# Down projection of a two-batch encoder: seven products over all tile pairs, two in turns, with splits and operand sums on VectorE

## The chip, the cores and the metric

The kernel runs on one core of one Trainium2 chip. The metric is the device time of one execution in microseconds; the profile is one execution of the same program, and its span is the time from the first to the last instruction. TensorE (PE in the profile) multiplies, VectorE (DVE), ScalarE (ACT) and GpSimd (POOL) do elementwise work, and SyncE (SP) issues nearly all transfers from one queue in order.

## The reference

A one-layer encoder with shared weights runs over two batches of 512 tokens with 1024 channels. Only its last part is touched here:

```python
    h = _rmsnorm(x, norm_ffn_g[l])
    gt, up = jnp.split(h @ w_gu[l], 2, axis=-1)
    x = x + (jax.nn.silu(gt) * up) @ w_down[l]
return _rmsnorm(x, final_norm_g)
```

D_FF is 2816, that is 22 tiles of 128. All is float32.

## The kernel before

**Precision.** A float32 operand is cut into a high part (a cast by ScalarE, L132) and a low part (source minus high part, a subtraction, L133). A product of two operands is three matmuls: high x high, high x low, low x high. `split` does the two instructions; the pair of results is called a block here.

**Two matrix products by Strassen and Winograd.** Gate and up, and then the down projection, are each computed as a 2 x 2 block product with seven products in the place of eight, from sums of the blocks (S of the left factor, T of the right one). In the down projection the left factor A is cut into (batch) x (halves of the 22 inner tiles), the right factor W into (halves of the inner tiles) x (halves of the 1024 outer channels). A *pair* p (0 to 10) is inner tile p together with inner tile p + 11. For a pair, A11 and A21 are the two batches of tile p, A12 and A22 those of tile p + 11, W11 and W12 the two halves of row tile p of w_down, W21 and W22 those of p + 11. The products are P1 = A11 W11, P2 = A12 W21, P5 = S1 T1, P6 = S2 T2, P3 = S4 W22, P7 = S3 T3, P4 = A22 T4, with S1 = A21 + A22, S2 = S1 - A11, S4 = A12 - S2, S3 = A11 - A21, T1 = W12 - W11, T2 = W22 - T1, T3 = W22 - W12, T4 = W21 - T2. One product of one pair is twelve matmuls of 512 columns: four token tiles, three each.

**The loop.** The eleven pairs go in three groups of 3, 4 and 4. In a group the seven products follow one another: P1, P2, P5, P6, P3, P7, P4. At the start of a group `d_raw` loads whole tiles (512 KB) of A, written to DRAM by gate and up as a_d, and of w_down. Functions c5, c6, c3, c7 and c4 make the sums in place on VectorE. Every third block takes its low part from GpSimd (`DLO = 'vvg'`), the others from VectorE. Four PSUM tiles (one per token tile) hold a product; X and Y sets of banks alternate. After a product, its sums leave PSUM: adds on VectorE into x2 (L1568, L1577, L1581, L1586, L1596), copies by ScalarE (L1565, L1572), and adds on GpSimd of these copies into x2 (L1573, L1578, L1582, L1583). In the last group the last product goes token tile by token tile, and `finish` does the last norm of a tile and writes it out.

**What sets the order.** Gate and up emits its products in a written order, one pair of column tiles after another. The program is then ordered for each engine by a scheduler with its own model of costs, so the order on the engines isn't that of the code. A tile with `bufs` buffers is a ring: a load into it waits until the last reader of the buffer's old content is done.

## Time and profile before

| what | us |
|---|---|
| three timed runs | 1886.22, 1885.33, 1880.94 (median 1885.33) |
| the profiled execution: time, span | 1886.2, 1886.2 |
| TensorE matmuls busy | 1748.8 (93%) |
| VectorE, ScalarE, GpSimd busy | 1177.0, 778.2, 785.5 |
| down projection, first matmul to last | 1604 to 1875 |

Times in the profile are from the start of the span. A timeline row has start, duration, engine, line, operation and tiles; a bracket at its end tells how long the engine was idle before it and what ended that. In groups, "x11 | 18.5, 1678" means 11 instructions, 18.5 us in all, 1678 ns each.

### The profile page before, as it was taken

To read this page: it belongs to the slowest core of one execution; us is meant where nothing else is said; L and a number is where in the kernel's file an instruction comes from. 1 tells how busy PE (TensorE), PEld (TensorE's weight loads), DVE (VectorE), ACT (ScalarE), POOL (GpSimd) and SP (SyncE) were. 2 spreads that over 40 slices of the span, in tenths; PEclk is the share of its full clock that TensorE was granted. 3 is DMA by queue.
4 is the path that set the end of the run, shared out by engine and by line. 5 is a ranking of instruction groups with operands and counts; after the bars stand their busy time and mean duration, and the time that the engine had idled before them with its cause. 6 is when DMAs were issued, how large, how long until landed. Compare 5 with 4: busy or idle time off the path is not lost.

```text
span 1886.2 us, 30967 instructions
## 1 busy us (share of the span) xinstructions
PE 1748.8 (93%) x11676; PEld 1372.1 (73%) x11676; DVE 1177.0 (62%) x1947; ACT 778.2 (41%) x1512; POOL 785.5 (42%) x1081
## 2 busy tenths in 40 slices
PE   6999999999999998899989998799999999778897
PEld 6887766777777775566658897588888888666675
DVE  6623554636445366877875557755555555898887
ACT  5534423343433436565643334333333333334345
POOL 3112436274463735251022136643333332647477
PEclk8999999999999998999999999899999999989998
DMA  4354443434434333220456630122222223430502
GB/s 166 125 171 152 117 115 85 121 88 113 114 87 119 88 104 105 62 54 17 168 199 204 190 101 12 45 90 90 78 90 79 89 79 118 173 112 1 178 1 89
DMA packets 174390, 197.44 MB, mean 105 GB/s; under 512 B 101600, under 2 KB 113248, under 8 KB 174240
## 3 DMA queue, kind: packets, MB, share of 16 engines
q1 hardware_dynamic: 173376, 193.95, 32.5%
q8 instruction: 92, 1.51, 0.3%
q10 hardware_dynamic: 720, 0.98, 0.2%
q14 instruction: 58, 0.48, 0.1%
q0 software_dynamic: 144, 0.52, 0.1%
HBM read 139.05 MB, written 56.36 MB: 104 GB/s over the span
## 4 chain that ended last, share of the span: by engine, by line
PE 64%; DVE 14%; DMA 8%; POOL 6%; issue 4%; ACT 2%; SPq 1%; DVEq 0%; POOLq 0%; ACTq 0%
PE pgC L125 9%; PE pj_gt L125 7%; PE pgB L125 6%; PE pgA L125 6%; PE pj_rkv L125 5%; PE s L125 2%; PE pdc L125 2%; PE pab L125 2%; PE pav L125 2%; DMA wor<-in_w_out 2%; PE sc L125 2%; PE pdx L125 2%; PE pj_mla L125 2%; POOL lt L839 2%; POOL el L841 2%
## 5 line engine op out<-in xcount | busy, mean ns | idle before, releaser
L839 POOL TENSOR_TENSOR lt<-lane,el 128x126 f32<-128x126 f32 (+22 forms) x248 | 94.6, 381 | 39.9 <-DMA lane<-nt_d 21.4
L841 POOL TENSOR_TENSOR el<-el,lt 128x126 f32<-128x126 f32 (+22 forms) x248 | 97.4, 393 | 19.0
L125 PE MATMUL pab<-yo,wab 128*128 128x512 f32 x384 | 94.5, 400 | 5.9 <-ACT yo L132 3.8
L125 PE MATMUL pj_gt<-h_hi,whi_gt 128*128 128x512 f32 x240 | 99.2, 413 | 0.0
L125 PE MATMUL pj_gt<-h_hi,wlo_gt 128*128 128x512 f32 x240 | 98.9, 412 | 0.2 <-DVE wlo_gt L133 0.2
L125 PE MATMUL pj_gt<-h_lo,whi_gt 128*128 128x512 f32 x240 | 98.1, 409 | 0.0
L1203 POOL TENSOR_TENSOR s<-uraw 128x512 f32<-128x512 f32 x22 | 29.2, 1329 | 158.5 <-DMA uraw<-in_w_gu 158.5
L125 PE MATMUL pwo<-woh,m 128*128 128x256 f32 x512 | 93.6, 283 | 0.0
L125 PEld LDWEIGHTS pab<-yo,wab 128*128 128x128 f32 x384 | 71.2, 190 | 26.3 <-DVE wab L133 4.5
L125 PEld LDWEIGHTS pwo<-woh,m 128*128 128x128 f32 x512 | 80.3, 192 | 0.3
L125 PE MATMUL pj_rkv<-h_hi,wlo_rkv 128*128 128x512 f32 x192 | 78.9, 414 | 0.0
L125 PE MATMUL pj_rkv<-h_lo,whi_rkv 128*128 128x512 f32 x192 | 78.1, 407 | 0.0
L125 PE MATMUL pj_rkv<-h_hi,whi_rkv 128*128 128x512 f32 x192 | 77.3, 403 | 0.0
L125 PE MATMUL pwo<-wol,m 128*128 128x256 f32 x256 | 72.5, 284 | 0.9 <-DVE wol L133 0.9
L1270 DVE TENSOR_TENSOR p<-p,pgC 128x512 f32<-128x512 f32 x22 | 15.1, 687 | 86.6 <-PE pgC L125 86.6
L1050 POOL TENSOR_TENSOR g<-g 128x512 f32<-128x512 f32 x16 | 24.9, 1559 | 93.0 <-DVE g L1048 81.8
L466 POOL TENSOR_SCALAR lut<-lut 128x512 f32<-128x512 f32 x32 | 20.5, 641 | 98.4 <-ACT lut L464 98.1
L919 ACT COPY sva<-s 64x128 f32<-64x128 f32 x64 | 16.5, 258 | 105.8 <-PE s L125 96.5
L920 DVE COPY svb<-s 64x128 f32<-64x128 f32 x64 | 18.8, 294 | 54.2 <-ACT sva L919 36.4
L1213 POOL TENSOR_TENSOR s<-graw,uraw 128x512 f32<-128x512 f32 x22 | 29.2, 1328 | 55.3 <-DVE S_2l L133 3.9
L125 PEld LDWEIGHTS pj_gt<-h_hi,wlo_gt 128*128 128x128 f32 x240 | 45.1, 188 | 9.6 <-DVE wlo_gt L133 0.9
L125 PE MATMUL sc<-kt,qh 128*128 128x512 f32 x128 | 50.9, 466 | 0.6 <-ACT pT L554 0.6
(1732 smaller groups left out, 5773.4 us busy)
## 6 DMA issues: line engine op xcount, KB each, us to landing
graw<-in_w_gu SPq DMA_DIRECT2D x22, 512.0 KB, 3.5
uraw<-in_w_gu SPq DMA_DIRECT2D x22, 512.0 KB, 3.6
araw<-a_d SPq DMA_DIRECT2D x22, 512.0 KB, 5.0
draw<-in_w_down SPq DMA_DIRECT2D x22, 512.0 KB, 4.9
a_d<-a SPq DMA_DIRECT2D x21, 512.0 KB, 3.3
x<-in_x SPq DMA_DIRECT2D x16, 512.0 KB, 8.2
rwkv_in<-lut SPq DMA_DIRECT2D x32, 256.0 KB, 2.1
gate_d<-gtt SPq DMA_DIRECT2D x32, 256.0 KB, 2.5
```

The lines of the kernel that those rows point to most:

```text
L125: pin(nc.tensor.matmul(out, lhsT, rhs, start=start, stop=stop, **kw), n if out.shape[0] > 64 else n / 2)
L466: nc.gpsimd.tensor_scalar(t, t, f, f, op0=ALU.mult, op1=ALU.add)
L839: eng.tensor_mul(lv, lane[:, s, s + 1:].unsqueeze(1).to_broadcast([P, m_, n]), el[:, 0:m_, s].unsqueeze(2).to_broadcast([P, m_, n]))
L841: eng.tensor_add(ev, ev, lv)
L919: nc.scalar.copy(sva[HA, :, c], s2[HA])
L920: nc.vector.tensor_copy(svb[HB, :, c], s2[HB])
L1050: nc.gpsimd.tensor_add(g_[:, 0], g_[:, 0], g_[:, 1])
L1203: vg(ES[min(j, 1)]).tensor_add(s1, a21, a22)
L1213: vg(ES[min(j, 1)]).tensor_sub(s3, a11, a21)
L1270: nc.vector.tensor_add(p1, p1, x_)
```

## The change

The groups go. Each product runs over all eleven pairs, and two products take turns, one pair of the one and then one of the other, on the two bank sets: P1 with P5, P6 with P3, P7 with P2, then P4 alone (its last four pairs token tile by token tile, as before). PSUM keeps P1 + P6 + P7 + P4 in X and P5 + P3 in Y running on, so that there are fewer evictions; the state after P1 and after P5 is copied out by ScalarE as before. S, T and W12 stay in SBUF for all pairs (11 buffers each), while the halves of A and W that a product needs are loaded by `d_half` when it needs them, 256 KB each, some of them twice. S3 is made in gate and up and written to DRAM (s3_d). All low parts and sums of the stage are VectorE's; GpSimd keeps eight adds, and its part of `finish`.

```diff
-GROUPS = ((0, 1, 2), (3, 4, 5, 6), (7, 8, 9, 10))
-DLO = 'vvg'
-DSE, DTE = 'v', 'v'
-DBLK = 8
+JP = NFF // 2
+NRH = 10
+DBLK = 7
+NLAST = 4
...
+    s3_d = [dram.tile([P, S], F32, name=f"s3_d{j}") for j in range(JP)]
...
         (nc.sync if j < NFF - 1 else nc.gpsimd).dma_start(a_d[j], a)
+        if j < JP:
+            nc.vector.tensor_sub(p5, a[:, 0], a[:, 1])
+            nc.sync.dma_start(s3_d[j], p5)
...
     lohalf, hihalf = slice(0, 512), slice(512, 1024)
-    cnt = [0, 0]
-    lop = DLO
-
-    def d_raw(tag, src, name):
-        raw = fp.tile([P, D], F32, tag=tag, bufs=2 * max(map(len, GROUPS)), name=name)
+    XB, YB = (3, 0), (1, 2)
+    cnt = [0]
+    def d_half(src, name):
+        raw = fp.tile([P, 512], F32, tag="rh", bufs=NRH, name=name)
         nc.sync.dma_start(raw, src)
         return raw
 
-    def d_block(src, name, first, eng=None):
-        pl, tag, bufs = (fw, "b", NBLK) if first else (fp, "d", DBLK)
+    def resident(tag, name):
+        return fp.tile([P, 512], F32, tag=tag, bufs=JP, name=name)
+    def d_block(src, name):
+        cnt[0] += 1
+        pl, tag, bufs = (fw, "b", NBLK) if cnt[0] % 2 else (fp, "d", DBLK)
         hi = pl.tile([P, 512], F32R, tag=f"{tag}hi", bufs=bufs, name=f"{name}h")
         lo = pl.tile([P, 512], F32R, tag=f"{tag}lo", bufs=bufs, name=f"{name}l")
-        cnt[0] += 1
-        split(hi, lo, src, vg(eng or lop[cnt[0] % len(lop)]))
+        split(hi, lo, src)
         return hi, lo
 
+    def banks(which, nm):
+        return [bank(which[t // 2], f"{nm}{t}") for t in range(4)]
+    def mms(ps, l, r, t, first):
+        ts = slice(t * P, (t + 1) * P)
+        mm3x(ps[t], l[0][:, ts], l[1][:, ts], r[0], r[1], start=first, stop=False, skip_group_check=True)
+    def prod_d(ps, l, r, first=False):
+        for t in range(4):
+            mms(ps, l, r, t, first)
+    def turns(fx, fy):
+        fx(0)
+        for p in range(1, JP):
+            fx(p)
+            fy(p - 1)
+        fy(JP - 1)
+    def xs(b, t, h):
+        return x2[b * 4 + t][:, (lohalf, hihalf)[h]]
...
-    fg = None
-    for gi, grp in enumerate(GROUPS):
...
-        def product(nm, ps, lhs, rhs, first, combos=None, touter=False):
-            blk = {}
-
-            def mms(p, t):
-                ts = slice(t * P, (t + 1) * P)
-                l, r = blk[p]
-                mm3x(ps[t], l[0][:, ts], l[1][:, ts], r[0], r[1], start=(first and p == grp[0]), stop=False,
-                     skip_group_check=True)
-            for p in grp:
-                if combos:
-                    combos(p)
-                early_ = gi == 0 and nm == "P1"
-                if early_ and p < 2:
-                    blk[p] = pre["araw"][1 + p], pre["draw"][1 + p]
-                else:
-                    blk[p] = [d_block(src[p], f"{nm}{k}{p}", early_ or touter and p < grp[2], "v" if early_ else None)
-                              for k, src in (("l", lhs), ("r", rhs))]
-                if not touter:
-                    for t in range(4):
-                        mms(p, t)
-            if touter:
-                yield -1
-                for t in range(4):
-                    for p in grp:
-                        mms(p, t)
-                    yield t
-
-        def go(*a, **kw):
-            for _ in product(*a, **kw):
-                pass
-
-        def xs(b, t, h):
-            return x2[b * 4 + t][:, (lohalf, hihalf)[h]]
-
-        SE, TE = vg(DSE), vg(DTE)
-
-        def c5(p):
-            SE.tensor_add(S_[p], A21[p], A22[p])
-            TE.tensor_sub(T_[p], W12[p], W11[p])
-
-        def c6(p):
-            SE.tensor_sub(S_[p], S_[p], A11[p])
-            TE.tensor_sub(T_[p], W22[p], T_[p])
-
-        def c3(p):
-            SE.tensor_sub(S_[p], A12[p], S_[p])
-
-        def c7(p):
-            SE.tensor_sub(A21[p], A11[p], A21[p])
-            TE.tensor_sub(W12[p], W22[p], W12[p])
-
-        def c4(p):
-            TE.tensor_sub(T_[p], W21[p], T_[p])
-        c = banks(0, "pdc")
-        go("P1", c, A11, W11, True)
-        p1 = [fp.tile([P, 512], F32, tag="p1", bufs=4, name=f"dp1{gi}{t}") for t in range(4)]
+    araw, W12, S_, T_ = {}, {}, {}, {}
+    X, Y = banks(XB, "dx"), banks(YB, "dy")
+    def p1_(p):
+        if p == 0:
+            araw[p], w11 = pre["araw"][0], pre["draw"][0][:, lohalf]
+        else:
+            araw[p] = fw_raw(a_d[p].rearrange("p b s -> p (b s)"), f"araw{p}")
+            w11 = d_half(w_down[p][:, lohalf], f"w11_{p}")
+        T_[p] = w11
+        if p < 2:
+            blk = pre["araw"][1 + p], pre["draw"][1 + p]
+        else:
+            blk = d_block(araw[p][:, lohalf], f"dA11_{p}"), d_block(w11, f"dB11_{p}")
+        prod_d(X, *blk, p == 0)
+    def p5_(p):
+        a22 = d_half(a_d[p + JP][:, 1], f"a22_{p}")
+        W12[p] = resident("w12", f"w12_{p}")
+        if p == 0:
+            nc.vector.tensor_copy(W12[p], pre["draw"][0][:, hihalf])
+        else:
+            nc.sync.dma_start(W12[p], w_down[p][:, hihalf])
+        w11, T_[p] = T_[p], resident("t", f"T{p}")
+        S_[p] = resident("s", f"S{p}")
+        nc.vector.tensor_add(S_[p], araw[p][:, hihalf], a22)
+        nc.vector.tensor_sub(T_[p], W12[p], w11)
+        blk = d_block(S_[p], f"dS1_{p}"), d_block(T_[p], f"dT1_{p}")
+        nc.vector.tensor_sub(S_[p], S_[p], araw[p][:, lohalf])
+        prod_d(Y, *blk, p == 0)
+    turns(p1_, p5_)
+    p1 = [fp.tile([P, 512], F32, tag="p1", bufs=4, name=f"dp1{t}") for t in range(4)]
+    p5 = [fp.tile([P, 512], F32, tag="p5", bufs=4, name=f"dp5{t}") for t in range(4)]
+    for t in range(4):
+        nc.scalar.copy(p1[t], X[t])
+    for t in range(4):
+        nc.scalar.copy(p5[t], Y[t])
+    w22 = {}
+    def p6_(p):
+        w22[p] = d_half(w_down[p + JP][:, hihalf], f"w22_{p}")
+        nc.vector.tensor_sub(T_[p], w22[p], T_[p])
+        blk = d_block(S_[p], f"dS2_{p}"), d_block(T_[p], f"dT2_{p}")
+        nc.vector.tensor_sub(W12[p], w22[p], W12[p])
+        prod_d(X, *blk)
+    def p3_(p):
+        a12 = d_half(a_d[p + JP][:, 0], f"a12_{p}")
+        nc.vector.tensor_sub(a12, a12, S_[p])
+        prod_d(Y, d_block(a12, f"dS4_{p}"), d_block(w22[p], f"dB22_{p}"))
+    turns(p6_, p3_)
+    for ps in (X, Y):
         for t in range(4):
-            nc.scalar.copy(p1[t], c[t])
-        go("P2", c, A12, W21, False)
-        for t in range(4):
-            nc.vector.tensor_add(xs(0, t, 0), xs(0, t, 0), c[t])
-        y = banks(1, "pdy")
-        go("P5", y, S_, T_, True, c5)
-        for t in range(4):
-            nc.scalar.copy(p5[t], y[t])
-            nc.gpsimd.tensor_add(p5[t], p5[t], p1[t])
-        x_ = banks(0, "pdx")
-        go("P6", x_, S_, T_, True, c6)
-        for t in range(4):
-            nc.vector.tensor_add(xs(0, t, 1), xs(0, t, 1), x_[t])
-            nc.gpsimd.tensor_add(xs(0, t, 1), xs(0, t, 1), p1[t])
-        go("P3", y, S_, W22, False, c3)
-        for t in range(4):
-            nc.vector.tensor_add(xs(0, t, 1), xs(0, t, 1), y[t])
-            nc.gpsimd.tensor_add(xs(1, t, 1), xs(1, t, 1), p5[t])
-            nc.gpsimd.tensor_add(xs(1, t, 0), xs(1, t, 0), p1[t])
-        go("P7", x_, A21, W12, False, c7)
-        for t in range(4):
-            nc.vector.tensor_add(xs(1, t, 1), xs(1, t, 1), x_[t])
-        for t in product("P4", x_, A22, T_, False, c4, touter=lastg):
-            if t < 0:
-                for i in range(4):
-                    finish(i)
-                continue
-            nc.vector.tensor_add(xs(1, t, 0), xs(1, t, 0), x_[t])
-            finish(4 + t)
-        if not lastg:
-            for t in range(4):
-                nc.vector.tensor_add(xs(1, t, 0), xs(1, t, 0), x_[t])
+            nc.vector.tensor_add(xs(0, t, 1), xs(0, t, 1), ps[t])
+    def p7_(p):
+        s3 = d_half(s3_d[p], f"s3_{p}")
+        prod_d(X, d_block(s3, f"dS3_{p}"), d_block(W12[p], f"dT3_{p}"))
+    Y = banks(YB, "dz")
+    def p2_(p):
+        a12, w21 = d_half(a_d[p + JP][:, 0], f"a12b{p}"), d_half(w_down[p + JP][:, lohalf], f"w21_{p}")
+        blk = d_block(a12, f"dA12_{p}"), d_block(w21, f"dB21_{p}")
+        nc.vector.tensor_sub(T_[p], w21, T_[p])
+        prod_d(Y, *blk, p == 0)
+    turns(p7_, p2_)
+    fg = fwr[0].tile([P, D], F32, tag="raw", bufs=NRAW, name="fg")
+    nc.sync.dma_start(fg, fng)
+    for t in range(4):
+        nc.vector.tensor_add(xs(1, t, 1), xs(1, t, 1), X[t])
+        nc.gpsimd.tensor_add(xs(1, t, 1), xs(1, t, 1), p5[t])
+    for t in range(4):
+        nc.vector.tensor_add(xs(0, t, 0), xs(0, t, 0), Y[t])
+        nc.gpsimd.tensor_add(xs(0, t, 0), xs(0, t, 0), p1[t])
+    def p4_(p):
+        a22 = d_half(a_d[p + JP][:, 1], f"a22b{p}")
+        return d_block(a22, f"dA22_{p}"), d_block(T_[p], f"dT4_{p}")
+    for p in range(JP - NLAST):
+        prod_d(X, *p4_(p))
+    last = [p4_(p) for p in range(JP - NLAST, JP)]
+    for t in range(4):
+        finish(t)
+    for t in range(4):
+        for blk in last:
+            mms(X, *blk, t, False)
+        nc.vector.tensor_add(xs(1, t, 0), xs(1, t, 0), X[t])
+        finish(4 + t)
 
 
 def layout(i):
```

Where the instructions stand now. VectorE at the start of the down projection, from its last row of gate and up (names: l and r in P1l2l are left and right factor, then pair, then l or h for the low or high part; dS1_0l is the low part of S1 of pair 0). Before:

```order
L1271 TENSOR_TENSOR a21_16050<-a21_16050,p1_21_15987 128x512
L133 TENSOR_TENSOR P1l2l_16202<-araw2_16146,P1l2h_16201 128x512
L133 TENSOR_TENSOR P1r2l_16206<-draw2_16148,P1r2h_16205 128x512
L1545 TENSOR_TENSOR S0_16167<-araw0_16111,araw11_16150 128x512
L1546 TENSOR_TENSOR T0_16168<-draw0_16117 128x512
L133 TENSOR_TENSOR P2l0l_16230<-araw11_16150,P2l0h_16229 128x512
L1556 TENSOR_TENSOR araw0_16111<-araw0_16111 128x512
L1557 TENSOR_TENSOR draw0_16117<-draw11_16152,draw0_16117 128x512
L133 TENSOR_TENSOR P2r0l_16234<-draw11_16152,P2r0h_16233 128x512
```

and with the change:

```order
L1272 TENSOR_TENSOR a21_16083<-a21_16083,p1_21_16020 128x512
L1527 COPY w12_0_16213<-draw0_16150 128x512
L1533 TENSOR_TENSOR T0_16215<-w12_0_16213,draw0_16150 128x512
L133 TENSOR_TENSOR dT1_0l_16224<-T0_16215,dT1_0h_16223 128x512
L1532 TENSOR_TENSOR S0_16216<-araw0_16144,a22_0_16211 128x512
L133 TENSOR_TENSOR dB11_2l_16249<-w11_2_16242,dB11_2h_16248 128x512
L133 TENSOR_TENSOR dS1_0l_16220<-S0_16216,dS1_0h_16219 128x512
L1535 TENSOR_TENSOR S0_16216<-S0_16216,araw0_16144 128x512
L133 TENSOR_TENSOR dA11_2l_16245<-araw2_16240,dA11_2h_16244 128x512
L1532 TENSOR_TENSOR S1_16269<-araw1_16195,a22_1_16264 128x512
L1533 TENSOR_TENSOR T1_16268<-w12_1_16266,w11_1_16197 128x512
L1532 TENSOR_TENSOR S2_16322<-araw2_16240,a22_2_16317 128x512
```

The splits of P1 and P2 and the sums of S and T stood there; now the copy of W12 of pair 0, then sums and splits of P5 and P1 in turns. The split of S1 of pair 10, the last operand of P5, stands 88 rows behind the copy.

GpSimd from the last store of gate and up on. Before:

```order
L1272 DMA a_d21_12232<-a21_16050 128x1024
L1583 TENSOR_TENSOR x2_4_10421<-x2_4_10421,dp100_16221 128x512
L133 TENSOR_TENSOR P2l1l_16250<-araw12_16154,P2l1h_16249 128x512
L1583 TENSOR_TENSOR x2_5_10422<-x2_5_10422,dp101_16222 128x512
L1583 TENSOR_TENSOR x2_6_10423<-x2_6_10423,dp102_16223 128x512
L1583 TENSOR_TENSOR x2_7_10424<-x2_7_10424,dp103_16224 128x512
L133 TENSOR_TENSOR P2r2l_16274<-draw13_16160,P2r2h_16273 128x512
L133 TENSOR_TENSOR P5l1l_16322<-S1_16169,P5l1h_16321 128x512
```

with the change:

```order
L1273 DMA a_d21_12232<-a21_16083 128x1024
L1582 TENSOR_TENSOR x2_4_10421<-x2_4_10421,dp50_16750 128x512
L1582 TENSOR_TENSOR x2_5_10422<-x2_5_10422,dp51_16751 128x512
L1582 TENSOR_TENSOR x2_6_10423<-x2_6_10423,dp52_16752 128x512
L1582 TENSOR_TENSOR x2_7_10424<-x2_7_10424,dp53_16753 128x512
L1585 TENSOR_TENSOR x2_0_10417<-x2_0_10417,dp10_16746 128x512
```

The splits and the adds of each group are gone; the adds that stand there now read sums of P7 and P2, five products later.

SP's queue at the same place, where the loads of the stage begin. Before:

```order
L1442 DMA araw1_16142<-a_d1_12212 128x1024
L1442 DMA draw1_16144<-in_w_down 128x1024
L1442 DMA araw2_16146<-a_d2_12213 128x1024
L1442 DMA draw2_16148<-in_w_down 128x1024
L1442 DMA araw11_16150<-a_d11_12222 128x1024
```

with the change:

```order
L1446 DMA w11_1_16197<-in_w_down 128x512
L1446 DMA a22_0_16211<-a_d11_12222 128x512
L1446 DMA w11_2_16242<-in_w_down 128x512
L1182 DMA araw2_16240<-a_d2_12213 128x1024
L1446 DMA a22_1_16264<-a_d12_12223 128x512
L1529 DMA w12_1_16266<-in_w_down 128x512
L1446 DMA w11_3_16295<-in_w_down 128x512
L1446 DMA a22_2_16317<-a_d13_12224 128x512
```

Whole tiles in group order have become halves in the order of use, and between them whole tiles of A (araw), which now share a ring of three buffers with the tiles of gate and up: araw2 takes the buffer of draw0, araw3 that of araw0, and so on by threes.

28 lines of the change are left out of this document (removed).

## The prediction

> **What bounds the kernel now.** I read the busy time by stretches first, for the whole kernel and then for the down projection. Columns: busy microseconds and instruction counts of TensorE (PE), its weight loads, VectorE (DVE), ScalarE (ACT), GpSimd (POOL), then granted clock, DMA share, GB/s.
>
> ```profile
> 1500.00:1600.00 100.00, 100.00 (x443) 82.81 (x442) 55.69 (x70) 34.00 (x58) 32.99 (x24) 1.00 0.28 93
> 1604.13:1875.14 271.01, 230.15 (x937) 183.13 (x935) 233.72 (x265) 110.51 (x209) 172.88 (x111) 0.94 0.23 86
> 1610.00:1620.00 10.00, 5.56 (x24) 3.92 (x22) 9.45 (x11) 5.77 (x11) 6.12 (x5) 0.99 1.03 407
> 1630.00:1640.00 10.00, 10.00 (x46) 8.27 (x45) 10.00 (x16) 3.94 (x7) 6.73 (x3) 1.00 0.00 0
> 1640.00:1650.00 10.00, 6.31 (x27) 4.55 (x26) 10.00 (x7) 2.19 (x5) 9.85 (x7) 1.00 0.01 2
> 1660.00:1670.00 10.00, 9.98 (x35) 8.06 (x36) 10.00 (x10) 3.33 (x7) 9.92 (x7) 0.80 0.41 157
> 1750.00:1760.00 10.00, 8.75 (x39) 6.89 (x37) 8.26 (x7) 6.33 (x12) 9.62 (x6) 1.00 0.61 213
> ```
>
> In the gate and up projection TensorE is full and VectorE half idle. In the down projection (1604 to 1875) it is the other way round. There VectorE does 16 instructions in ten microseconds when GpSimd is moderately busy and 7 when GpSimd is full, and calls itself full both times. The timeline of the two engines side by side shows why (start, duration, instruction):
>
> ```profile
> 1614.26 0.68 DVE L133 TENSOR_TENSOR P2l0l<-araw,P2l0h 128x512 fp32r<-128x512 f32 x1
> 1614.86 1.77 DVE L1556 TENSOR_TENSOR araw<-araw 128x512 f32<-128x512 f32 x1
> 1616.55 1.76 DVE L1557 TENSOR_TENSOR draw<-draw,draw 128x512 f32<-128x512 f32 x1
> 1618.23 1.75 DVE L133 TENSOR_TENSOR P2r0l<-draw,P2r0h 128x512 fp32r<-128x512 f32 x1
> ...
> 1626.64 0.68 DVE L133 TENSOR_TENSOR P2r1l<-draw,P2r1h 128x512 fp32r<-128x512 f32 x1
> 1627.24 0.68 DVE L1545 TENSOR_TENSOR S<-araw,araw 128x512 f32<-128x512 f32 x1
> ...
> 1660.49 1.87 DVE L1577 TENSOR_TENSOR x<-x,pdx 128x512 f32<-128x512 f32 x3
> ```
>
> ```profile
> 1614.65 1.43 POOL L1583 TENSOR_TENSOR x<-x,dp 128x512 f32<-128x512 f32 x1 [1.64 <-ACT dp L1565]
> 1616.05 1.71 POOL L133 TENSOR_TENSOR P2l1l<-araw,P2l1h 128x512 fp32r<-128x512 f32 x1
> 1617.72 5.08 POOL L1583 TENSOR_TENSOR x<-x,dp 128x512 f32<-128x512 f32 x3
> ```
>
> Alone, a split or a sum starts every 0.60 us (1626.64 to 1627.24). Beside a GpSimd instruction it starts every 1.69 us (1614.86 to 1616.55), so one GpSimd instruction takes 1.09 us from VectorE. The adds that read PSUM (L1577, three in 1.87 us, in a stretch with GpSimd 9.92 of 10) aren't stretched. What that does to TensorE, in the chain of waits (first row) and in its timeline:
>
> ```profile
> 1601.41 2.72 PE pgC L125 x12
> ```
>
> ```profile
> 1620.03 0.79 PE L125 MATMUL pdc<-P2r0l,P2l0h 128*128 128x512 f32 x1 [4.48 <-DVE P2r0l L133]
> 1620.62 0.63 PE L125 MATMUL pdc<-P2r0h,P2l0l 128*128 128x512 f32 x1
> 1621.05 0.63 PE L125 MATMUL pdc<-P2r0h,P2l0h 128*128 128x512 f32 x1
> ...
> 1627.38 0.50 PE L125 MATMUL pdc<-P2r1l,P2l1h 128*128 128x512 f32 x1 [2.21 <-DVE P2r1l L133]
> ...
> 1874.75 0.39 PE L125 MATMUL pdx<-P4r10h,P4l10l 128*128 128x512 f32 x1
> ```
>
> Twelve matmuls of 512 columns take 2.72 us, 0.227 each. After 4.48 us of idleness they are 0.43 apart for a while, after 2.21 us they aren't.
>
> The floor of the stage follows. It has 924 matmuls (7 products x 11 pairs x 12), and the last 12 of gate and up lie between them: 78 twelves x 2.72 = 212.2 us. From 1604.1 that ends at 1816.3. It ends at 1875.0 now (the last starts at 1874.75), so at most **58.7 us** can be won. The last norm behind it, from there to the end of the span at 1886.2, is 11.2 us and isn't changed.
>
> **The change part by part.** *GpSimd's work.* Of its 111 instructions between 1604 and 1875, the splits and 40 of 48 adds go; 8 adds, the products by fg and the small powers stay, all in the last product. Before that nothing of GpSimd runs in this stage, so VectorE's rows cost 0.60 us there.
>
> *VectorE's rows.* In the changed order 89 rows (the copy of W12 to the split of S1 of pair 10) lie between its last row of gate and up and the operands of the last P5. That row of gate and up and a ScalarE cast:
>
> ```profile
> 1611.24 0.69 DVE L1271 TENSOR_TENSOR a<-a,p 128x512 f32<-128x512 f32 x1
> 1606.71 0.62 ACT L132 CAST P1l2h<-araw 128x512 fp32r<-128x512 f32 x1 [2.10 <-PE pdc L125]
> ```
>
> VectorE is free at 1611.9. 89 x 0.60 = 53.4 brings it to 1665.3. To this come two casts at the start that it must wait for (2 x 0.65 = 1.3), and loads. The bound is one copy SBUF to SBUF that the trace of before lacks at this size with both ends there; I price it as any row, and it can't cost less than nothing or more than a stretched row's 1.77.
>
> *Loads.* The list of transfers of the whole kernel, and that of the time from 1604 on, when many are under way (KB each, us to landing):
>
> ```profile
> uraw<-in_w_gu SPq DMA_DIRECT2D x22, 512.0 KB, 3.6
> araw<-a_d SPq DMA_DIRECT2D x21, 512.0 KB, 5.1
> ```
>
> SP's queue is in order. araw2 takes the place of draw0, so it waits for T of pair 0 (done at about 1613.0), and everything behind it waits too: a22_1, w12_1, w11_3 and so on. It lands at 1613.3 + 3.6 = 1616.9, is cast by 1617.5, and VectorE wants it at 1616.9: 0.6 us (2.1 by the 5.1 us under load; nothing else is under way then, so I take the first). The pieces behind it arrive 0.65 us apart at the 407 GB/s of the row above (256 KB each); a22_2 is the third half behind it, and VectorE waits another 1.2. Later each araw(p+3) waits for the last use of araw(p); by the rows between, only araw8 is late, by 0.9. In all 2.7. Nine loads of 512 KB and 37 of 256 KB, 14.4 MB, in some 55 us are 262 GB/s. That lies between the 407 and the 213 of the rows above. By 407 the 2.7 stands; by 213 the loads take 68 us, and 12 us are added. I take 2.7, since the 213 was a stretch where the loads waited for buffers, and keep 12 for the range.
>
> Sum of this part: 1665.3 + 1.3 + 2.7 = 1669.3. P5 of pair 9 gets its split two rows before and starts at about 1668.8, P5 of pair 10 follows at 1671.5 and ends at **1674.3**. TensorE alone, from its first P5 at about 1616.2 (five rows and two casts after 1611.9), would need 20 x 2.72 = 54.4 and end at 1670.6: the two engines are nearly level, and VectorE leads by little. That is the lower bound.
>
> *The other five products.* 55 x 2.72 = 149.6 us. VectorE has 164 rows there, 98 us at 0.60, or 7 rows (4.2 us) for every 5.44 us of TensorE in P6 and P3, where they are densest. TensorE is the bound, at 1674.3 + 149.6 = 1823.9. The evictions are 20 adds on VectorE where 60 stood; P6 may write X's banks only after four ScalarE copies, P7 and P4 only after four adds. In the built order two products of the other bank pair (5.44 us) lie between, against 4 x 0.6 us. I cost them at nothing; without that cover they are 2.4 us each, 7.2 in all.
>
> *GpSimd in the last product.* From the end of P7, VectorE has 25 rows of 512 elements (15.0 us), about 1 us of small ones, and up to 16 GpSimd instructions (8 adds, 8 products by fg) that take 1.09 each: 33.4 at most. TensorE gives it 5.44 (two products of P2), 7 x 2.72, and some 2 us until the last block is needed: 26.5. So 0 to 6.9; I take 3, because the products by fg come late, behind ScalarE.
>
> The Trainium skill, SBUF — State Buffer, "Who interferes with whom", says that the pair of ports that VectorE and GpSimd share is locked for a whole instruction and the loser blocks. GpSimd's instruction alone is 1.29 us here, in the groups of the time from 1400 to 1600:
>
> ```profile
> L1203 POOL TENSOR_TENSOR s<-uraw 128x512 f32<-128x512 f32 x10 | 12.9, 1290 | 80.9 <-DMA uraw<-in_w_gu 80.9
> ```
>
> By the page's lock the bound of 6.9 would be 16 x 0.20 = 3.2 us larger. The 1.69 against 0.60 of VectorE's own rows decides.
>
> *Gate and up.* Eleven tile pairs get one subtraction and one 256 KB store more. Their cover:
>
> ```profile
> L1271 DVE TENSOR_TENSOR a<-a,p 128x512 f32<-128x512 f32 x11 | 18.5, 1678 | 0.0
> L1270 DVE TENSOR_TENSOR p<-p,pgC 128x512 f32<-128x512 f32 x11 | 7.6, 687 | 43.9 <-PE pgC L125 43.9
> L1261 DVE TENSOR_TENSOR e<-e,pgB 128x512 f32<-128x512 f32 x10 | 6.9, 687 | 15.6 <-PE pgB L125 15.6
> ```
>
> VectorE waits 4.0 us per pair for TensorE at L1270 and 1.5 at L1261, and the new row takes 0.6 to 1.7 just ahead of the second wait. The store is queued on SP one row later than the store of a and ahead of the next load of uraw, so it holds SP up by no more than the subtraction takes. TensorE has no pause in the stretch from 1500 to 1600 that stands at the top. I cost it at nothing; without that cover it is 11 x 1.77 = 19.5.
>
> *The sum*: 1823.9 + 3.0 + 11.2 = 1838.1, and 1 us for matmuls on half clock after an idle stretch. **1839 us** against the profiled 1886.2, which is 0.9 above the median of the three runs, so 47 us or 2.5%.
>
> The Trainium skill, TensorE: Matmul & The Clock Gate, "HAM oscillation", wants no idle gap over about 3.4 us. The trace agrees: 2.21 us left the clock alone, 4.48 didn't. The changed first part may have two gaps of 3 to 4 us (before P1 of pairs 2 and 4); if the page counts them, each makes some 8 matmuls 0.2 us longer, 3.2 us in a part that VectorE sets anyway.
>
> **The rivals.** *Loads set the first part.* The loads are smaller, more, and chained through buffers. For it: SP's queue waits for VectorE before most of these loads, and the margins are a few microseconds. Against: 407 GB/s in the trace. By the 213 row 12 us more: 1851; with P6's loads late too, up to 1862.
>
> *TensorE without a gap.* VectorE's rows overlap the waits that I added, and the last product's stall vanishes: 1816.3 + 11.2 = 1827.5. For it, only that the engines are nearly level; against, the 4.3 us of operands that have to be made before the first P5.
>
> *VectorE becomes the bound of everything, and it is slower than before.* All 253 rows up to the last split are now on VectorE. If the stretching doesn't come from GpSimd but from ScalarE, or from the transfers, whose share rises, the rows stay at 1.69. 253 x 1.69 = 428 us from 1611.9 is 2040, + 11.2 = 2051. It decides from a mean of (1875.0 - 1611.9) / 253 = 1.04 us per row. Against: at 1614.26 the row is still 0.68, with the DMA at 407 GB/s and ScalarE at work; it stretches when GpSimd starts at 1614.65.
>
> *No change.* The gain is there, but in-order waits of VectorE for block buffers (5 on the left side) take it back: 1886. The five-block lead is 2.5 pairs, 13 us; I find no row that would be waited for that long.
>
> **How the numbers follow.** Forecast, 1832 to 1846: 0.58. Loads, 1846 to 1862: 0.22. No gap, under 1832: 0.10. Slower than before: 0.04. No change, or a part of the gain (above 1862): 0.06, half of it within 0.3% of before, which is about what a measurement of this kernel can tell from no change. That makes faster 0.93, the same 0.03, slower 0.04. The range is 1828 to 1860: it takes in the gapless bound and the loads at 213 GB/s with most of what can follow.
>
> **What would show it.** Right: no GpSimd tensor instruction from about 1612 to the end of P7, VectorE's rows at 0.68, busy share of TensorE near full from the start of P6, and a first part that ends near 1674 with short waits of TensorE on VectorE's splits. Loads: SP waits on VectorE, VectorE idle until araw or a22 lands. Wrong as a whole: rows of VectorE above 1.04 us without GpSimd beside them, or TensorE idle in P6 to P7.

## The result, and the profile after

| | kernel before | changed kernel |
|---|---|---|
| device time, median (lowest to highest) of 4 runs, us | 1885.09 (1880.94 to 1886.22) | 1834.53 (1830.80 to 1838.51) |
| ratio, 95% interval | | 0.9737 [0.9718, 0.9757] |
| the profiled execution: time, span, us | 1886.22, 1886.2 | 1835.74, 1834.0 |
| first P1 matmul starts, us | 1603.97 | 1600.02 |
| last matmul starts, us | 1874.75 | 1825.73 |
| between them | 270.8 | 225.7 |
| from there to the end of the span | 11.4 | 8.3 |

The changed kernel is 2.6% faster: 50.6 us between the medians, where 47 were forecast. Of the 52.2 us between the two spans, 45.1 come from the down projection, 3.2 from what lies behind its last matmul, and 4.0 from the program ahead of it, which has no part in the change (the last section shows that this start moves by itself).

The busy time by stretches of the changed kernel answers to the first table of the prediction (TensorE, its weight loads, VectorE, ScalarE, GpSimd, then granted clock, DMA share, GB/s):

```profile
1600.02:1825.73 225.71, 216.44 (x936) 177.34 (x935) 171.88 (x270) 105.36 (x197) 30.68 (x24) 0.98 0.44 147
1620.00:1630.00 10.00, 7.41 (x32) 5.47 (x30) 10.00 (x18) 4.61 (x9) 0.00 (x0) 1.00 1.04 390
1630.00:1640.00 10.00, 8.97 (x32) 7.25 (x33) 9.54 (x16) 4.46 (x8) 0.00 (x0) 0.83 0.98 362
1640.00:1650.00 10.00, 10.00 (x45) 8.27 (x45) 10.00 (x18) 3.87 (x7) 0.00 (x0) 1.00 0.39 123
1750.00:1760.00 10.00, 10.00 (x46) 8.29 (x45) 6.56 (x10) 4.29 (x8) 0.00 (x0) 1.00 0.45 140
1810.00:1820.00 10.00, 7.81 (x33) 5.83 (x33) 6.30 (x7) 4.20 (x10) 8.25 (x6) 1.00 0.28 110
```

GpSimd does no arithmetic in the stage until P7 is done (its first addition starts at 1787.19). VectorE does 18 rows in ten microseconds in which it calls itself full, where it did 7 beside GpSimd. TensorE is full in every window of ten microseconds from 1640 to 1810, of which two are shown. What it lacks is at the two ends: the waits of TensorE in the whole stage are five (line of the waiting instruction, what it waited for: us, times, longest):

```profile
PE dy L125 <- ACT dS_0h L132: 3.5, 1, 3.5
PE dx L125 <- ACT dA_4h L132: 2.2, 1, 2.2
PE dx L125 <- ACT dA_10h L132: 1.6, 1, 1.6
PE dx L125 <- ACT dA_3h L132: 1.4, 1, 1.4
PE dx L125 <- DVE dA_9l L133: 0.6, 1, 0.6
```

Three of them, 7.1 us, lie in the first part (P1 and P5 in turns), two, 2.2 us, in the last product. The timeline gives the cuts used in all that follows, the first P1, the first P6 and the last matmul: the first part takes 73.6 us, the rest 152.1.

```profile
1600.02 0.39 PE L125 MATMUL dx<-P1drawh,P1arawh 128*128 128x512 f32 x1
...
1673.60 0.39 PE L125 MATMUL dx<-dT_0h,dS_0h 128*128 128x512 f32 x1
...
1825.73 0.39 PE L125 MATMUL dx<-dT_10h,dA_10l 128*128 128x512 f32 x1
```

The chain of waits shows where the first part is late. It goes through one transfer after the other to the cast of the left block of pair 4:

```profile
1612.26 6.04 DMA w<-in_w_down
...
1618.36 5.95 DMA a<-a_d
...
1624.37 5.96 DMA araw<-a_d
...
1630.36 0.63 ACT dA_4h L132
...
1631.03 3.10 PE dx L125 x8
```

No row of VectorE stands in it. Each transfer takes 6 us to land and is issued right when the one ahead in the chain has landed, while the loads run at 390 GB/s (the window from 1620).

### The profile page after: what moved, and what is told of

Read it like the earlier page. It is cut to its first block, busy times and chain, and to the rows that moved or that the text cites. A ratio compares the mean times of both kernels' runs of the same rounds, so it can differ in the third digit from the quotient of the medians.

```text
span 1834.0 us, 31000 instructions
## 1 busy us (share of the span) xinstructions
PE 1734.3 (95%) x11676; PEld 1365.7 (74%) x11676; DVE 1116.9 (61%) x1957; ACT 771.0 (42%) x1496; POOL 642.2 (35%) x992
## 4 chain that ended last, share of the span: by engine, by line
PE 70%; DVE 9%; DMA 8%; POOL 5%; issue 3%; ACT 2%; SPq 1%; DVEq 0%; POOLq 0%; ACTq 0%
PE pgC L125 9%; PE pj_gt L125 8%; PE pgB L125 6%; PE pgA L125 6%; PE pj_rkv L125 5%; PE dx L125 5%; PE dy L125 3%; PE s L125 3%; PE pab L125 2%; PE sc L125 2%; PE pav L125 2%; PE pj_mla L125 2%; DMA wor<-in_w_out 2%; PE o L125 2%; PE gx L125 2%
## 5 line engine op out<-in xcount | busy, mean ns | idle before, releaser
L1203 POOL TENSOR_TENSOR s<-uraw 128x512 f32<-128x512 f32 x22 | 29.3, 1330 | 152.1 <-DMA uraw<-in_w_gu 152.1
L1582 POOL TENSOR_TENSOR x<-x,dp 128x512 f32<-128x512 f32 x4 | 6.3, 1590 | 178.1 <-DVE x L1581 178.1
L125 PEld LDWEIGHTS pj_gt<-h_hi,wlo_gt 128*128 128x128 f32 x240 | 45.1, 188 | 9.5 <-DVE wlo_gt L133 0.8
L125 PEld LDWEIGHTS pj_gt<-h_hi,whi_gt 128*128 128x128 f32 x240 | 45.1, 188 | 8.6
L125 PEld LDWEIGHTS pj_gt<-h_lo,whi_gt 128*128 128x128 f32 x240 | 45.1, 188 | 8.4
```

Source lines behind the costliest of these rows:

```text
L125: pin(nc.tensor.matmul(out, lhsT, rhs, start=start, stop=stop, **kw), n if out.shape[0] > 64 else n / 2)
L1203: vg(ES[min(j, 1)]).tensor_add(s1, a21, a22)
L1582: nc.gpsimd.tensor_add(xs(1, t, 1), xs(1, t, 1), p5[t])
```

## The experiments

The theory: GpSimd's instructions took VectorE's time in the down projection, and the gain is their going. The rivals: the new order and its fewer evictions are the gain; loads, not VectorE, set the first part; each row or GpSimd instruction costs its price wherever it stands. All ratios below are to the kernel before on the same chip, so they compare with 0.9737.

| kernel | median us | ratio [95%] | first part | first P6 to last matmul | whole stage | behind it |
|---|---|---|---|---|---|---|
| changed kernel | 1834.53 | 0.9737 [0.9718, 0.9757] | 73.6 | 152.1 | 225.7 | 8.3 |
| b_splits | 1863.30 | 0.9904 [0.9888, 0.9921] | | | 253.6 | 10.3 |
| b_allv | 1847.56 | 0.9820 [0.9806, 0.9835] | | | 235.0 | 14.2 |
| b_noadds | 1836.84 | 0.9762 [0.9738, 0.9785] | | | 219.9 | 14.8 |
| a_third | 1848.45 | 0.9828 [0.9803, 0.9854] | 86.6 | 149.8 | 236.4 | 11.8 |
| a_dose | 1882.25 | 1.0008 [0.9994, 1.0021] | 73.7 | 197.5 | 271.2 | 8.2 |
| a_paced | 1833.87 | 0.9743 [0.9719, 0.9768] | 73.5 | 152.1 | 225.6 | 8.3 |
| a_dosecp | 1847.81 | 0.9817 [0.9794, 0.9840] | 72.2 | 154.1 | 226.3 | 20.3 |
| a_vdose | 1837.48 | 0.9751 [0.9734, 0.9768] | 74.8 | 152.1 | 226.9 | 8.2 |
| a_noaraw | 1831.43 | 0.9722 [0.9707, 0.9736] | 67.9 | 152.2 | 220.1 | 8.3 |
| a_s2 | 1829.22 | 0.9712 [0.9698, 0.9726] | 67.9 | 152.2 | 220.1 | 8.1 |
| a_adds | 1831.91 | 0.9724 [0.9708, 0.9740] | 72.3 | 149.4 | 221.6 | 8.2 |
| a_both | 1823.04 | 0.9688 [0.9669, 0.9707] | 67.5 | 149.4 | 216.8 | 8.1 |

The stage columns come from one profiled execution each: starts of the first P1, first P6 and last matmul, and the span's end. The first part is the same work in a_dose, a_dosecp, a_paced, a_adds and the changed kernel and takes 72.2 to 73.7 us there, so a difference of 1.5 says nothing. (The two at 72.2 and 72.3 have one stretch of half clock in it, the other three have two; the last section tells why this varies.)

### What the gain is made of: b_splits, b_allv, b_noadds

b_splits moves GpSimd's splits in the kernel before to VectorE, b_allv its additions too. b_noadds is b_allv without the 32 additions of kept sums in the first two groups, so these sums are missing from its output.

```diff
-DLO = 'vvg'
+DLO = 'vvv'
```
```diff
-            nc.gpsimd.tensor_add(p5[t], p5[t], p1[t])
+            nc.vector.tensor_add(p5[t], p5[t], p1[t])
...
-            nc.gpsimd.tensor_add(xs(1, t, 0), xs(1, t, 0), p1[t])
+            nc.vector.tensor_add(xs(1, t, 0), xs(1, t, 0), p1[t])
```
```diff
-            nc.gpsimd.tensor_add(p5[t], p5[t], p1[t])
+            if lastg:
+                nc.vector.tensor_add(p5[t], p5[t], p1[t])
...
```

> The kernel before, with the one edit that every low part of the down projection is made on VectorE (none on GpSimd); its 48 additions stay on GpSimd, the order of the products stays. By my theory (each GpSimd instruction takes 1.09 us from VectorE, which bounds the stage, and a row of VectorE alone costs 0.60) 50 splits go: + 50 x 0.60 - 50 x 1.09 = -24 us, so about 1861 us, within 1855 to 1872 since TensorE bounds some stretches. Rival (the gain lies in the order in turns and in the fewer evictions): no change, 1885, or slower by up to 30 us, since VectorE has 50 rows more.

> The kernel before, with all splits and all 48 additions of the down projection on VectorE, its old order of products and its 60 evictions kept. By my theory 98 GpSimd instructions go: VectorE has some 350 rows x 0.60 = 210 us, level with TensorE's 212, so the stage takes 225 to 235 us in place of 271: 1840 to 1855 us, and what then is left to the changed kernel (5 to 20 us) is the worth of its order and of its 40 evictions less. Rival (GpSimd is all): 1835, the same as the changed kernel. Rival (the order is what counts): above 1870.

> The kernel before with all its work in the down projection on VectorE, in its old order, and with the 32 additions of kept sums of the first two groups left out, so these sums are missing from the output, which isn't the reference's. It asks what the changed kernel's remaining lead over the all-VectorE kernel of the old order is made of (from the first P1 to the last matmul 235.0 against 225.7 us). If VectorE's number of rows sets the stage there, 32 x 0.60 = 19 us of VectorE go and the 15 us that TensorE waits at the starts of products shrink to 6 or less: 225 to 229 us for the stage, about 1840. If the order sets it (each product starts with operands and banks that stand behind the additions of the one before), the 28 evictions still in the way keep the waits: 232 to 235 us, 1845 to 1848.

b_splits came out 18 us under the kernel before (ratio 0.9904), where 24 were expected, and b_allv 34 under it (0.9820): both inside what the theory gave, and both far from the rivals. VectorE has 50 rows more in b_splits and is done sooner. So some 34 of the 50 us are GpSimd leaving the stage, with the old order of the products. In b_allv TensorE's waits stand at the starts of products or one pair behind them, 15 us; the longest two:

```profile
PE pdx L125 <- DVE x L1586: 5.4, 3, 3.5
PE pdx L125 <- DVE P6r0l L133: 3.0, 1, 3.0
```

In b_noadds the first of them is down to 1.6 us (the same line, four lower there), and the four waits that are left make 5.6 us:

```profile
PE pdx L125 <- DVE x L1590: 1.6, 2, 0.9
```

The stage of b_noadds is 219.9 us, less than the forecast 225 to 229, and less than the changed kernel's 225.7. So it is the number of VectorE's rows that stood behind those waits, not the old order: with 32 rows fewer the old order keeps TensorE fuller than the changed kernel does (5.6 us of waits and no stretch of half clock, against 9.3 us and two). Against b_allv the changed kernel is 9.3 us shorter in the stage and 5.9 behind it (8.3 us against 14.2). The 9.3 are put down to its fewer additions and evictions, which accumulating over all eleven pairs makes possible; the changed kernel itself was not run with the old number of them. What the turns as such are worth was not tried alone either.

### What one GpSimd instruction costs: a_dose, a_paced, a_third, a_dosecp

```diff
+    junk = fp.tile([P, 512], F32, tag="fj", bufs=1, name="dose")
+    for i in range(66):
+        nc.gpsimd.tensor_add(junk, p1[i % 4], p5[i % 4])
     turns(p6_, p3_)
```

> The changed kernel with 66 additions on GpSimd added at the start of P6, each of two finished tiles into a scratch tile that nobody reads; no other edit, and the result isn't touched. They run back to back for about 105 us, while VectorE has 78.9 us of work in the 116.8 us of P6, P3, P7 and P2. By my theory each takes 1.09 us from VectorE: 78.9 + 72 = 151, 34 us more than TensorE needs; with the pitch of 1.69 us only some 62 rows are stretched, which gives 27. So 1861 to 1869 us, TensorE idle behind VectorE's splits. If a GpSimd instruction takes its own full time (the Trainium skill, SBUF - State Buffer, "Who interferes with whom": the port pair is locked for a whole instruction), 78.9 + 66 x 1.29 = 164, so 47 more: 1882. Rival (the stretching came from transfers or from ScalarE): 1834.5.

It took all the gain back: 47.7 us over the changed kernel, ratio 1.0008. The timeline of VectorE beside the 66 additions, and the one row of GpSimd:

```profile
1674.07 110.95 POOL L1562 TENSOR_TENSOR dose<-dp,dp 128x512 f32<-128x512 f32 x66 [64.28 <-ACT dp L1544]
...
1679.41 1.78 DVE L133 TENSOR_TENSOR dS_1l<-a,dS_1h 128x512 fp32r<-128x512 f32 x1
1681.11 1.77 DVE L133 TENSOR_TENSOR dB_2l<-w,dB_2h 128x512 fp32r<-128x512 f32 x1
...
1783.81 1.87 DVE L1566 TENSOR_TENSOR x<-x,dy 128x512 f32<-128x512 f32 x3
```

VectorE's rows are 1.70 us apart, so one GpSimd addition takes 1.10 us from it; the prediction had 1.09. The additions that read PSUM (L1566) run at 0.6 us beside it, again as before. The price held, and the sum of 27 to 34 us made with it did not. It set the whole slack of P6 to P2 against the dose, but the dose stands in P6 and P3 alone. There, 108.5 us pass from the first P6 (1674.44) to the first P2 (1782.95), which are 24 twelves or 65 us for TensorE; what slack VectorE has in the rest of P7 and P2 comes too late to help. The Trainium skill, SBUF — State Buffer, "Who interferes with whom", gave + 47, which is the time that came out, but by the same sum over the whole slack. Its lock for a whole instruction would put the rows 0.60 + 1.29 = 1.89 us apart, and they are 1.70; the measured pitch decides.

a_paced puts 22 additions where VectorE has room, spread by what they read:

```diff
         nc.vector.tensor_sub(T_[p], w21, T_[p])
+        junk = fp.tile([P, 512], F32, tag="fj", bufs=1, name=f"dose{p}")
+        for i in range(2):
+            nc.gpsimd.tensor_add(junk, T_[p], p5[i])
```

> The changed kernel with 22 additions on GpSimd into a scratch tile that nobody reads, two per pair of P2, each held back until T of that pair is made, so that they are spread over P7 and P2 (59.8 us), where VectorE has 5 rows (3.0 us) for TensorE's 5.44 us. My theory after the 66 additions in a row: a GpSimd instruction takes 1.10 us from VectorE, and it costs the end only where VectorE has no room in that very stretch: 3.0 + 2.2 = 5.2 of 5.44, so 0 to 2 us, TensorE without a gap from P6 to P2. Rival (each costs its price wherever it stands): + 24 us.

No cost: 0.9743 against 0.9737. The list of TensorE's waits has four of the five rows of the changed kernel with the same lengths (that for the cast of dA_3h is absent), and no other. The additions run from 1708.4 to 1772.2 in pairs; eight of them begin while TensorE is still in P6 and P3, the others in P7 and P2. The rows beside them are stretched all the same:

```profile
1742.78 0.69 DVE L133 TENSOR_TENSOR dS_4l<-s,dS_4h 128x512 fp32r<-128x512 f32 x1
1743.38 1.79 DVE L133 TENSOR_TENSOR dT_5l<-w,dT_5h 128x512 fp32r<-128x512 f32 x1
1745.10 1.78 DVE L133 TENSOR_TENSOR dA_3l<-a12b,dA_3h 128x512 fp32r<-128x512 f32 x1
```

So the same instruction costs 0 or 0.7 us (47.7 / 66) at the end, by where it stands and how many stand together.

a_third undoes one part of the change:

```diff
-        split(hi, lo, src)
+        split(hi, lo, src, vg('vvg'[cnt[0] % 3]))
```

> The changed kernel, with every third low part of the down projection back on GpSimd (50 splits), and nothing else changed. By my theory 50 splits cost VectorE 50 x (1.09 - 0.60) = 24 us in sum, but most of it falls in the five products in which VectorE has slack (78.9 of 116.8 us busy from the start of P6 to the end of P7 and P2); only the first part (13 splits, about +6) and the last product (7 splits, +3) show it: 1839 to 1845 us. Rival (every GpSimd instruction costs its price wherever it stands): 1859. Rival (the gain came from the order alone): 1834.5.

1848.45 us, 14 over the changed kernel, outside the 1839 to 1845 expected. The five later products hide their part, as expected (149.8 us from P6 on, even 2.3 less than without). The first part grew by 13.0 us and not by 6, and the reason is another one than a price per instruction:

```profile
1644.82 7.08 POOL L133 TENSOR_TENSOR dB_9l<-w,dB_9h 128x512 fp32r<-128x512 f32 x1 [4.25 <-ACT dB_9h L132]
...
1666.86 8.79 POOL L133 TENSOR_TENSOR dA_10l<-araw,dA_10h 128x512 fp32r<-128x512 f32 x1 [4.92 <-ACT dA_10h L132]
...
1649.47 0.68 DVE L1552 TENSOR_TENSOR w<-w,w 128x512 f32<-128x512 f32 x1
1650.07 0.68 DVE L133 TENSOR_TENSOR dS_6l<-S,dS_6h 128x512 fp32r<-128x512 f32 x1
1654.63 0.69 DVE L1557 TENSOR_TENSOR a<-a,S 128x512 f32<-128x512 f32 x1 [3.88 <-DMA a<-a_d]
```
```profile
PE dx L125 <- POOL dA_10l L133: 5.6, 1, 5.6
```

Here it is GpSimd that waits. A split that takes 1.26 us alone lasts 7.08 while VectorE's rows beside it run on, 0.60 us apart; it ends 1.15 us after VectorE has stopped for a load. The split of pair 10 lasts 8.79 in the same way, and TensorE waits 5.6 us for it. Work given to GpSimd in a stretch where VectorE is full is not only paid by VectorE, it may come late itself.

a_dosecp asks whether it is the two operands. It has the edit of a_dose with

```diff
+        nc.gpsimd.tensor_copy(junk, p5[i % 4])
```

> The changed kernel with 66 copies on GpSimd (SBUF to SBUF, one operand, 128x512, f32) into a scratch tile that nobody reads, at the same place as the 66 additions. It asks whether GpSimd's instructions with one operand take VectorE's time as those with two do. If it is the engine that counts, VectorE's rows stretch as before, by 1.1 us or by a copy's own length: + 30 to 48 us. If it is the two operands, VectorE's rows stay at 0.60 us: 1834.5.

```profile
1673.34 57.03 POOL L1562 COPY dose<-dp 128x512 f32<-128x512 f32 x57 [62.77 <-ACT dp L1544]
...
1678.69 1.09 DVE L133 TENSOR_TENSOR dS_1l<-a,dS_1h 128x512 fp32r<-128x512 f32 x1
1679.71 1.09 DVE L133 TENSOR_TENSOR dB_2l<-w,dB_2h 128x512 fp32r<-128x512 f32 x1
...
1806.18 7.18 POOL L1562 COPY dose<-dp 128x512 f32<-128x512 f32 x7
1823.66 1.09 POOL L1493 TENSOR_TENSOR frs<-frs,mhalf 128x1 f32<-128x1 f32 x2 [10.30 <-DVE frs L1491]
```

Neither answer fits. Rows are 1.02 us apart beside copies of 1.00 us each, so a copy takes 0.42 us of VectorE's time where an addition takes 1.10. The 13 us of this kernel are not the copies' price in P6, for from the first P6 to the last matmul it is only 2.0 us longer. The end behind the last matmul grew by 12 us. Nine copies stand in the last product, but they are through at 1813.4, and GpSimd then waits 10.3 us for a row of VectorE before the first small power of the last norm, which started at 1801.16 in the changed kernel. So the scheduler put the last norm behind nearly all of the last product here. That it did so because of the copies is likely and not shown.

### Who sets the first part: a_vdose, a_noaraw, a_s2

a_vdose adds a row of VectorE per pair, a_noaraw leaves out the loads of eight left tiles (their pairs compute with the tile of an earlier pair), a_s2 makes S2 elsewhere.

```diff
+        junk = fp.tile([P, 512], F32, tag="fj", bufs=1, name=f"dose{p}")
+        nc.vector.tensor_sub(junk, T_[p], S_[p])
         blk = d_block(S_[p], f"dS1_{p}"), d_block(T_[p], f"dT1_{p}")
```
```diff
-            araw[p] = fw_raw(a_d[p].rearrange("p b s -> p (b s)"), f"araw{p}")
+            araw[p] = fw_raw(a_d[p].rearrange("p b s -> p (b s)"), f"araw{p}") if p < 3 else araw[p - 2]
```
```diff
-        nc.vector.tensor_sub(S_[p], S_[p], araw[p][:, lohalf])
...
+        a22, s3 = d_half(a_d[p + JP][:, 1], f"a22c{p}"), d_half(s3_d[p], f"s3c{p}")
+        nc.vector.tensor_sub(S_[p], a22, s3)
         w22[p] = d_half(w_down[p + JP][:, hihalf], f"w22_{p}")
```

> The changed kernel with 11 more rows on VectorE in the first part (P1 and P5 in turns), one per pair: the difference of T1 and S1 into a scratch tile that nobody reads; the result isn't touched, loads as before. It asks who sets the first part, which takes 73.6 us from the first P1 to the first P6 in the trace of the changed kernel. If VectorE leads there, as my prediction had it, 11 x 0.60 = 6.6 us go to the end: about 1841 us. If TensorE and the loads lead there, as the trace of the changed kernel looks (three gaps of TensorE in the first 30 us, none after), VectorE has room until the rows are more than TensorE's 5.44 us per pair: 9 rows become 10, 6.0 against 5.44, so 0 to 4 us, the first part 74 to 77 us.

> The changed kernel without the 512 KB loads of the left side (araw) from pair 3 on: these eight pairs take the tile of an earlier pair, so this part of the product is computed from other data and the output isn't the reference's; the instructions of VectorE, ScalarE and TensorE are the same in number. It prices the loads of the first part. If loads make the gaps of TensorE before P1 of pairs 3 and 4 (1.4 and 2.2 us) and the clock loss behind them, the first part takes 69 to 71 us in place of 73.6, and the time is about 1831. If VectorE sets the part, it stays at 73 or more, since its rows are the same: 1834.

> The changed kernel with S2 = A22 - S3 made in P6 from two more loaded halves, in place of S1 - A11 in the first part. It takes 11 rows (6.6 us) from VectorE in the first part, frees the araw tiles one step earlier, and puts 11 rows and 22 loads of 256 KB into P6, where VectorE then has 8 rows (4.8 us) for TensorE's 5.44 per pair of P6 and P3. My theory: the first part shrinks by 2 to 4 us by either cause, P6 to P2 stay without a gap: 1831. Rival (P6's loads come late, or 4.8 in 5.44 is too tight): the first part shrinks and P6 loses 3 to 8 us: 1834 to 1840.

Eleven rows more on VectorE (6.6 us) made the first part 1.2 us longer, which is within what it varies by. Without the 512 KB loads from pair 3 on it is 5.7 us shorter (4.3 against the shortest first part with the same work), with VectorE's rows unchanged in number, and TensorE's waits before P1 of pairs 3 and 4 are gone: only the 3.5 us before the first P5 stay. So the loads set the first part, on top of TensorE's own work, and VectorE has room. a_s2 reaches the same 67.9 us with all loads made: the left tiles come free one step earlier, and their loads stand earlier on SP's queue. Its timeline shows it: the load for pair 4 is the third here, issued 17.0 us after the first P1 (1598.42), where it was 24.4 us in the changed kernel (1624.37 against 1600.02).

```profile
1607.53 0.32 SPq L1182 DMA_DIRECT2D araw<-a_d  x1
1610.22 0.39 SPq L1182 DMA_DIRECT2D araw<-a_d  x1
1615.37 0.33 SPq L1182 DMA_DIRECT2D araw<-a_d  x1
```

a_s2 also has eleven rows of VectorE less in the first part, but a_vdose shows that such rows are worth little there. P6 carries its eleven more rows and 22 more loads without a gap (152.2 us).

### The last product, and the version that beats both: a_adds, a_both

```diff
         nc.vector.tensor_sub(T_[p], w21, T_[p])
         prod_d(Y, *blk, p == 0)
+        if p < 4:
+            nc.vector.tensor_add(xs(1, p, 1), xs(1, p, 1), p5[p])
+            nc.vector.tensor_add(xs(0, p, 0), xs(0, p, 0), p1[p])
...
-        nc.gpsimd.tensor_add(xs(1, t, 1), xs(1, t, 1), p5[t])
...
-        nc.gpsimd.tensor_add(xs(0, t, 0), xs(0, t, 0), p1[t])
```

> The changed kernel with the 8 additions of the kept sums of P1 and P5 made by VectorE in the middle of P7 and P2, where it has 5 rows (3.0 us) for 5.44 us of TensorE, in place of GpSimd's additions in the last product. My theory of the last product: GpSimd's 8 additions stretch 7 rows there; without them the 0.6 us that TensorE waits for a split goes, the 1.6 us behind ScalarE's queue (its cast stands behind a scaling that waits for GpSimd's small power, which stands behind the products by fg) may stay: 1832 to 1834.5, that is 0.6 to 2.2 us, which the time can't tell but the trace can. Rival (rows in P7 and P2 push TensorE): slower by 1 to 5.

Both waits of the last product are gone, also the 1.6 us behind ScalarE that were expected to stay: from the first P6 to the last matmul it is 149.4 us, and 55 twelves of 2.72 are 149.6. P7 and P2 take the eight rows without a gap. The time (0.9724) can't be told from the changed kernel's.

a_both joins a_s2 and a_adds, and puts the copy of W12 of pair 0 behind the operands of the first P5:

```diff
-        if p == 0:
-            nc.vector.tensor_copy(W12[p], pre["draw"][0][:, hihalf])
-        else:
+        w12 = W12[p] if p else pre["draw"][0][:, hihalf]
+        if p:
             nc.sync.dma_start(W12[p], w_down[p][:, hihalf])
...
         blk = d_block(S_[p], f"dS1_{p}"), d_block(T_[p], f"dT1_{p}")
+        if not p:
+            nc.vector.tensor_copy(W12[p], w12)
```

> The changed kernel with three edits: S2 = A22 - S3 made in P6 from loaded halves; the 8 additions of the kept sums on VectorE inside P7 and P2; and for pair 0 the copy of W12 put behind the operands of the first P5. My theory: the first shortens the first part by 5.7 us, the second closes TensorE's gaps in the last product (2.2 to 2.8 us), the third starts the first P5 0.4 to 0.6 us earlier, and they add: 8 to 9 us less than the changed kernel, ratio to the kernel before about 0.969, 1825.5 us. Rival (P6 with 8 rows and P7 with one row more per pair for four pairs get gaps): 0.971 to 0.973.

1823.04 us, ratio 0.9688, as expected (0.969): 3.1% under the kernel before and 0.5% under the changed one. One wait of TensorE is left in the stage:

```profile
PE dy L125 <- ACT dS_0h L132: 3.0, 1, 3.0
```

## Why the prediction was right, and where it was not

**The time.** 1839 us were forecast with a gain of 47; 1834.5 and 50.6 came. The sum was made against the profiled 1886.2, and in that execution the program ahead of the stage was 4.0 us later than in the profile after. In the stage itself the forecast gain was 47.1 and 45.1 came; what was missing was given back by the end, which the prediction took as unchanged and which became 3.2 us shorter. That the forecast is nearer than its parts is luck.

**GpSimd's price and VectorE's rows: right.** 0.60 us alone, 1.69 beside, 1.09 for one GpSimd instruction, additions from PSUM untouched: a_dose measures 1.70 and 1.10, and the rows of the changed kernel stand 0.60 apart in the stage until GpSimd begins at 1787. The rival by which the rows stay stretched would have shown above 1.04 us.

**The first part: its length was 3.4 us off, and the step that failed is "VectorE leads by little".** 70.2 us were forecast (1604.1 to 1674.3), 73.6 came. The rows of VectorE were counted rightly, but it was not they that were late: the split of S1 of pair 10, forecast for 1669.3, was done at 1666.3, 4.6 us before TensorE came to that pair (1670.88). TensorE led, and its time is its own 62.6 us (23 twelves), three waits of 7.1 and 3.9 that are left, most of it half clock (some 15 matmuls 0.43 apart in place of 0.23 are 3.0); the forecast of TensorE alone (1670.6, that is 66.5) had one wait of 4 us in it. a_vdose shows VectorE's room, a_noaraw that two of the waits and the half clock behind the second are loads. The prediction had 2.7 us of loads, put on VectorE; they cost 4.3 to 5.7, on TensorE, the half clock that they bring included. It followed each left tile to the buffer that it waits for, and said that only that of pair 8 is late. What it did not count is what stands ahead of the left tile on SP's queue by then: W12 and the halves of later pairs, which have eleven and ten buffers. Between the issues for pair 3 (1615.65) and pair 4 (1624.37) SP issued 11 halves, 2.9 MB, which are 7 us at the 390 GB/s of the time. The buffer for pair 4 was free at 1620.67 (end of VectorE's last row that reads it), so its load stood 3.7 us behind others with nothing else to wait for. It was the mechanism of the rival "loads set the first part", at less than half of its 12 us.

**The clock: mis-sized.** 1 us was taken for half clock and 3 to 3.9 came, in the first part alone. The rule of the Trainium skill that the prediction weighed (TensorE: Matmul & The Clock Gate, "HAM oscillation") gave 3.2 us for two gaps, in a part that VectorE was to set; since TensorE set it, the loss came in full. The two gaps were told for P1 of pairs 2 and 4, at 3 to 4 us each. They came before the first P5 (3.46) and before P1 of pair 4 (2.18), so that the amount agrees is in part luck.

**The other five products: right.** TensorE has no wait from P6 to the end of P7 and P2, and the evictions cost nothing.

**GpSimd in the last product: the size right, the cause half wrong.** 3 us were taken, and 2.2 of waits came. But only 0.6 is a stretched split. The 1.6 is ScalarE: the cast of pair 10 stands in its queue behind a scaling of the last norm, which waits for a small power on GpSimd, which stands behind the products by fg. The chain of waits of the changed kernel:

```profile
1812.58 1.74 POOL x L1498
1814.32 0.97 POOL frs L1493
...
1815.94 0.71 ACT x L1497
1816.64 0.52 ACT dA_10h L132
...
1817.21 6.21 PE dx L125 x26
```

a_adds, which takes out GpSimd's eight additions that stand ahead of these products, closes both waits.

**Gate and up: right.** The extra subtraction and store cost nothing: from the first row of the addition ahead of a to the last, 387.4 us pass in both profiles (each row gives the starts of the first and the last, after first):

```profile
L1271 DVE TENSOR_TENSOR p<-p,pgC x22: 686/687/689, 1219.2 to 1606.6; 128x512 f32<-128x512 f32 x22
```
```profile
L1270 DVE TENSOR_TENSOR p<-p,pgC x22: 686/686/689, 1223.1 to 1610.5; 128x512 f32<-128x512 f32 x22
```

**The end: taken as unchanged, 3.2 us shorter.** In the profile before, two of the last scalings of VectorE stand beside GpSimd's products by fg and take 3.47 us. In the profile after GpSimd is through with them by then, and two take 1.33 in the chain. The add of the last token tile stands behind them in VectorE's order. It starts 0.43 us after the last matmul (1826.16), where it was 3.64 us (1878.39), and this is the 3.2.

```profile
1872.01 3.47 DVE L1471 SCALAR_TENSOR_TENSOR x<-x,frs,fg 128x512 f32<-128x512 f32 x2 [0.28 <-POOL frs L1464]
```

## What to carry to other kernels

Price a shared resource by the distance between starts of the engine that loses it, and then set that price against the slack of the very stretch in which the instruction runs: 66 additions in a row, in the two products with the least room, cost 48 us; 22 spread over 64 us with room cost nothing. Where a part is forecast from the engine with the most rows, also write down what stands on the load queue ahead of each transfer that a matmul needs; here transfers for later pairs, which had free buffers, went ahead of one that was needed first. And before a move to another engine is credited to a new order, make that move alone: with the old order it gave 34 of the 50 us.
